# Making the first tile's branch products, y and transposed y in the end of the last attention unit

## The chip, the core and the metric

The kernel runs on one core of a Trainium2 chip. The metric is the device time of one execution in microseconds (us). The core's engines work side by side, each through a list of its own: PE (matrix multiplication, with PEld for the loading of weights), DVE (vector), ACT (activation functions), POOL (general purpose) and SP, which here only issues DMA transfers (its rows are called SPq). They wait for each other through semaphores.

## What is computed

One layer of a streaming encoder, for 2048 prompt rows and 8 x 16 sample rows of width 1024. Rows are normalized and projected; then come two kinds of attention, a differential softmax attention (4 heads) and a stick-breaking attention (8 heads, weights from a running product along the keys); then the two results are merged:

```python
oa = rms_norm(oa, subln_g) * (1.0 - lam_init)
ya = (oa.reshape(b, s, WIDTH_A) * jax.nn.silu(za)) @ w_branch_a
yb = (ob.reshape(b, s, WIDTH_B) * jax.nn.silu(zb)) @ w_branch_b
return (jax.nn.sigmoid(ga) * ya + jax.nn.sigmoid(gb) * yb) @ w_out
```

The merged rows are gated, added to the input and normalized. The sample rows also attend to caches of 512 keys and values for each of 8 sequences. Keys and values are outputs too.

Every product of high precision is made of three fp16 matmuls: each operand is cut into a high and a low half (`split`: the high half is a cast, on ACT or POOL, and the low half is what is left, on DVE, L294), and high x high, high x low and low x high are added up in PSUM.

## The kernel before, in words

There are three stages.

**Stage 0** normalizes the rows and writes them, transposed, to DRAM.

**Stage 1, attention.** Eight units (u = 0 to 7), each a head of the softmax kind or two heads of the stick-breaking kind, go over 17 tiles of 128 rows each: the sample tile first, then the 16 prompt tiles. A loop of 138 iterations (136 steps, and two more for what is left) issues the pieces of each: projections some tiles ahead, taken from one long list, the scores of this tile (`scores`), and the weighted sums of the values of the tile two steps back (`pv`). For a stick-breaking head a chunk of 512 keys goes through PE (L628, L629), two sigmoids on ACT (L119), a scan on DVE (L605), and for each stretch of 1024 keys a product on POOL (L611), a cast on ACT (L561), a subtraction on DVE (L562) and a transposing DMA into `wt` (L569), which PE then uses in L680 and L681. Unit 7 is of the stick-breaking kind, and its last tiles are the longest: 15 and 16 blocks of keys.

When the list of projections has run out, which happens some four iterations before the end, `early_work` makes another short list: the last of the branch weights, the handing out of buffers (`rest`), and `inputs` of the first two tiles of stage 2. It is spread evenly over the iterations that are left.

**Stage 2, the output.** The pools of stage 1 are closed, and their memory goes to the buffers of stage 2. Tile by tile:

- `inputs(t)` loads o, z (into two buffers, `hs0` and `hs1`) and the gates g, makes o * silu(z) on POOL (L1144), ACT (L119) and DVE (L1150, L1146), and splits it into `u16` (`hs2`).
- `turned` transposes u on PE (L1126, two groups of eight), and ACT copies it from PSUM (L1127).
- `branches` makes four products of 12 matmuls each (L1268, half j and branch br); DVE scales and gates each (L1270), POOL adds the two branches (L1272), and `finish` makes y: squares on ACT (L271), the scale in a few column operations on DVE, two splits, and `iy` (L1286).
- `turned_y` transposes y as `turned` does.
- `output` makes two products of 24 matmuls with `wo`, the cut w_out (L1309), and then the gate, the addition of x (L1317), the last normalization and the store (L1323).

In iteration n of the output loop stand the branches of tile n, `turned` of tile n + 1, `inputs` of tile n + 2, `output` of tile n - 1 and `turned_y` of tile n, interleaved by their stated costs with the pieces of the sample lane, `aside(n)`: the sample rows' attention to the caches (L727 loads, L734 transposing DMAs, L752 scores, L783 weighted sums), about five steps of it beside each of the first tiles. Ahead of the loop the eight pieces of w_out are loaded and cut (L1118, with two buffers, then L291 or L289 and L294).

PSUM has two banks for branch products and sigmoids of z (`mm`), three for scores and transposes (`s`), one `t` and two `o`.

A scheduler goes over all this: it keeps the order in which buffers are handed out, but may move an instruction ahead of others on its engine by its own estimate of time. So the compiled order of each engine is fixed, and it isn't that of the source. On one engine the instructions start in that order.

Of the kernel before, what the change touches and what calls it, by code (L numbers as in the profile page):

```python
# [16 lines left out]
F32 = mybir.dt.float32  # L17
F16 = mybir.dt.float16
# [3 lines left out]
ALU = mybir.AluOpType  # L22
# [3 lines left out]
P = 128  # L26
# [83 lines left out]
def layer_kernel(ctx: ExitStack, tc: tile.TileContext, a: dict):  # L110
# [74 lines left out]
    def bank(tag, dt=F32):  # L185
        return ps.tile([P, 512 if dt == F32 else 1024], dt, tag=tag, name=f"ps_{tag}", bufs=BANKS[tag])
# [26 lines left out]
    def scales(square, pool, name, n=1):  # L213

        tag = "sc" if n == 1 else f"sc{n}"
        kw = {} if n == 1 else dict(bufs=1)
        q = tiny.tile([P, n], F32, tag=tag + "_q", name="sc_q", **kw)
        V.tensor_scalar(out=q, in0=square, scalar1=2.0 ** -46, scalar2=None, op0=ALU.max)
        f = tiny.tile([P, n], I32, tag=tag + "_f", name="sc_f", **kw)
        V.tensor_scalar(out=f, in0=q.bitcast(I32), scalar1=24, scalar2=None, op0=ALU.logical_shift_right)  # L220
        e = tiny.tile([P, 2 * n], I32, tag=tag + "_e", name="sc_e", **kw)
        V.tensor_scalar(out=e[:, 0:n], in0=f, scalar1=-1.0, scalar2=204.0, op0=ALU.mult, op1=ALU.add)
        V.tensor_scalar(out=e[:, n : 2 * n], in0=f, scalar1=50.0, scalar2=None, op0=ALU.add)
        s = pool.tile([P, 2 * n], I32, tag=name, name=name)
        V.tensor_scalar(out=s, in0=e, scalar1=23, scalar2=None, op0=ALU.logical_shift_left)
        return s.bitcast(F32)
# [39 lines left out]
    def sum_squares(src, n, dst, width=1024, scale=1.0):  # L266

        for i in range(0, n, width):
            junk = tiny.tile([P, width], F16, tag="junk", name="junk", bufs=1)
            w = min(width, n - i)  # L270
            S.activation(out=junk[:, 0:w], in_=src[:, i : i + w], func=AF.Square, scale=scale,  # L271
                         accum_out=dst[:, i // width : i // width + 1])

    def add_up(acc, n):
        if n == 1:
            return acc[:, 0:1]
        col = tiny.tile([P, 1], F32, tag="col", name="col")
        V.tensor_reduce(out=col, in_=acc[:, 0:n], axis=AX.X, op=ALU.add)
        return col
# [6 lines left out]
    def split(hi, lo, src, s, on=None):  # L286

        if on is S:
            S.activation(out=hi, in_=src, func=AF.Identity, scale=s)  # L289
        elif on is G:  # L290
            G.tensor_scalar(out=hi, in0=src, scalar1=s, scalar2=0.0, op0=ALU.mult, op1=ALU.add)  # L291
        else:
            V.tensor_scalar(out=hi, in0=src, scalar1=s, scalar2=None, op0=ALU.mult)
        V.scalar_tensor_tensor(out=lo, in0=src, scalar=s, in1=hi, op0=ALU.mult, op1=ALU.subtract)  # L294
# [818 lines left out]
    L = {}  # L1113
# [8 lines left out]
    def transposed(x16, dst, half):  # L1122

        pt = bank("s", F16)
        for k in range(KT):
            T.transpose(pt[:, k * P : (k + 1) * P], x16[:, half, k * P : (k + 1) * P], id16)  # L1126
        S.copy(out=dst[:, half * KT : (half + 1) * KT, :], in_=pt.rearrange("p (k n) -> p k n", n=P))  # L1127
# [34 lines left out]
    def turned(st):  # L1162

        st["u"] = st["u"].bitcast(F16).rearrange("p (k n) -> p k n", n=P)
        for half in range(2):
            transposed(st["u16"], st["u"], half)


    tiles = list(range(NT - 1)) + [NT, NT - 1]
    states, begun = {}, []  # L1170
# [14 lines left out]
    def early_work():  # L1185


        free.extend(units[7]["bufs"])

        def first(t):  # L1190
            if "orms" not in L:
                L["orms"] = rsqrt(osums[:, 0:NT, :].rearrange("p t h -> p (t h)"), 4 * NT, P, con, "orms")
            states[t] = inputs(t)
            if t == tiles[0]:
                turned(states[t])

        def rest():
            L["g"], L["u"], (L["y"], L["y16"]) = free[0:4], free[4:6], free[6:8]

        return [branch_weight for _ in branch_weights] + [rest] + [lambda t=t: first(t) for t in tiles[0:2]]  # L1200

    for n in range(len(steps) + PV_LAG):
        made, qk, vs = [], [], []
# [30 lines left out]
    with ExitStack() as c2:  # L1234
# [21 lines left out]
            T.matmul(pg, sel[0:9, i * P : (i + 1) * P], gsm[0:9, :], start=True, stop=True)  # L1256
            return pg

        def branches(st):

            def half(j, br):
                c = slice(j * 512, (j + 1) * 512)
                g = st["g"][j][:, br, :]
                pb = bank("mm")
                n = 0
                for wi, ui in ((0, 0), (0, 1), (1, 0)):
                    for k in range(4):
                        T.matmul(pb, st["u"][:, ui * 8 + br * 4 + k, :], wb[br * 4 + k // 2 * 2 + j][:, wi, k % 2, :], start=(n == 0), stop=(n == 11))  # L1268
                        n += 1
                V.scalar_tensor_tensor(out=g, in0=pb, scalar=st["iu"], in1=g, op0=ALU.mult, op1=ALU.mult)  # L1270
                if br == 1:
                    G.tensor_tensor(out=g, in0=st["g"][j][:, 0, :], in1=g, op=ALU.add)  # L1272
                    if j == 1:
                        finish()

            def finish():
                acc = tiny.tile([P, 2], F32, tag="yacc", name="yacc")
                for j in range(2):
                    sum_squares(st["g"][j][:, 1, :], 512, acc[:, j : j + 1])
                sy = scales(add_up(acc, 2), unit, "sy")  # L1280
                y16 = L["y16"].bitcast(F16).rearrange("p (f n) -> p f n", f=2)
                for j in range(2):
                    c = slice(j * 512, (j + 1) * 512)
                    split(y16[:, 0, c], y16[:, 1, c], st["g"][j][:, 1, :], sy[:, 0:1], S)
                iy = unit.tile([P, 1], F32, tag="iy", name="iy")
                V.tensor_tensor(out=iy, in0=sy[:, 1:2], in1=s_o[:, 1:2], op=ALU.mult)  # L1286
                st["y16"], st["iy"] = y16, iy

            return [(2.6, lambda j=j, br=br: half(j, br)) for j in range(2) for br in range(2)]

        def turned_y(st):
            st["y"] = yT = L["y"].bitcast(F16).rearrange("p (k n) -> p k n", n=P)
            for half in range(2):
                transposed(st["y16"], yT, half)

        def output(t, st):
            box = {}

# [47 lines left out]
        load(out=fg, in_=a["final_g"].rearrange("(o d) -> o d", o=1).to_broadcast([P, D]))  # L1346
        for n in range(NT + 2):
            work = []
            if n <= NT:
                work += branches(states[tiles[n]])  # L1350
            if n + 1 <= NT:

                work.insert(2, (0.9, lambda n=n: turned(states[tiles[n + 1]])))
            if n + 2 <= NT:
                work.insert(5, (0.1, lambda n=n: states.update({tiles[n + 2]: inputs(tiles[n + 2])})))
            if n > 0:
                work += output(tiles[n - 1], states.pop(tiles[n - 1]))
            if n <= NT:
                work.append((0.9, lambda n=n: turned_y(states[tiles[n]])))
            interleave(work, aside(n))  # L1360

# [26 lines left out]
```

## Time and profile before

| | |
|---|---|
| median of 3 runs | 2374.07 us (2372.82 to 2374.98) |
| profiled execution | 2379.63 us, its span 2377.8 us |
| granted PE clock, mean of the span | 0.959 |
| PE busy | 2115.9 us (89%) |
| DVE busy | 1736.5 us (73%) |
| ACT busy | 1658.8 us (70%) |
| POOL busy | 749.0 us (32%) |
| last weighted sum of attention (L681) | 1823.02 us |
| first output product (L1309) | 1872.30 us |

Times inside the span count from its start. In the page's second part the span is cut into 40 slices of 59.4 us, and a digit gives the busy share of an engine in tenths; PEclk is the clock that was granted to PE. In a timeline a row has its start, its length, engine, line, operation, what it writes and reads, the count of merged instructions, and in brackets the idle time before it with what ended it. Lengths of pipelined matmuls overlap: the pace of a group is the distance from its start to that of the next. In a table by windows each engine has its busy time and the number of its instructions, and the last three columns are the granted clock, the share of the DMA engines' time and GB/s.

### The profile page before, as it was taken

How to read it: one execution, taken by the hardware profiler on the slowest of the kernel's cores; microseconds unless marked ns; L12 is line 12 of the kernel's file. 1: busy time of each engine (PE TensorE's matmuls, PEld its weight loads, DVE VectorE, ACT ScalarE, POOL GpSimd, SP SyncE). 2: the span in 40 equal slices, each digit the busy share in tenths (PEclk: the TensorE clock that was granted, in tenths of full speed). 3: DMA queues.
4: the chain of work that ended last, by engine and by line, in shares of the span. 5: the costliest groups of instructions: out<-in, count | busy, mean ns of one | idle time of the engine just before them, and what ended most of it. 6: DMA issues, size and time to landing. Idle time of an engine off the chain costs nothing. (4 is left out here: it accounts for less than half of the span.)

```text
span 2377.8 us, 42492 instructions
## 1 busy us (share of the span) xinstructions
PE 2115.9 (89%) x15136; PEld 1126.4 (47%) x15136; DVE 1736.5 (73%) x3647; ACT 1658.8 (70%) x3216; POOL 749.0 (32%) x604
## 2 busy tenths in 40 slices
PE   5779998998989899899999989999986779888998
PEld 2435554444545445445545544554543344444443
DVE  4868665779875667977667797777787777777654
ACT  3758767787886777877677787866776767766652
POOL 1833022345300233641023364103343333232322
PEclk7979999999999999999999999999997889999899
DMA  9668859887795878878687897866788999999421
GB/s 325 223 197 213 204 132 242 191 197 160 186 237 129 201 187 191 175 181 186 145 196 181 182 181 180 193 155 153 155 185 198 271 247 244 233 252 227 147 99 54
DMA packets 843573, 453.74 MB, mean 191 GB/s; under 512 B 538234, under 2 KB 786346, under 8 KB 842848
## 3 DMA queue, kind: packets, MB, share of 16 engines
q1 hardware_dynamic: 843360, 451.03, 77.0%
q8 instruction: 118, 1.93, 0.3%
q14 instruction: 95, 0.78, 0.1%
HBM read 249.80 MB, written 73.44 MB: 136 GB/s over the span
## 5 line engine op out<-in xcount | busy, mean ns | idle before, releaser
L611 POOL TENSOR_TENSOR sc_p<-sc_p,sc_n 128x127 f32<-128x127 f32 (+7 forms) x192 | 308.6, 1611 | 900.5 <-DVE sc_n L605 887.5
L426 PE MATMUL ps_mm<-wb,hs 128*128 128x512 f16 x1632 | 413.1, 381 | 0.2 <-DVE v L294 0.2
L426 PEld LDWEIGHTS <-hs 128*128 128x128 f16 x3120 | 271.9, 98 | 258.1 <-DMA hs<-hT_d 17.1
L426 PE MATMUL ps_mm<-wa,hs 128*128 128x512 f16 x1488 | 373.4, 383 | 15.1 <-DMA hs<-hT_d 15.1
L605 DVE TENSOR_TENSOR_SCAN sc_n<-ps_s,sc_n,zero_t 128x512 f32<-128x512 f32 x192 | 245.4, 1278 | 80.2 <-ACT ps_s L119 76.0
L628 PE MATMUL ps_s<-k,qst 128*128 128x512 f16 (+3 forms) x640 | 225.8, 354 | 45.4 <-DVE sc_n L605 38.7
L562 DVE TENSOR_TENSOR sc_n<-sc_p,sc_n 128x128 f16<-128x128 f32 (+7 forms) x192 | 224.4, 1172 | 54.4 <-ACT sc_n L561 53.8
L493 PEld LDWEIGHTS <-hs 128*128 128x128 f16 x1632 | 156.1, 98 | 183.1 <-DVE qst L521 5.6
L119 ACT ACTIVATE sc_p<-ps_s,usc 128x512 f32<-128x512 f32 (+3 forms) x320 | 202.8, 634 | 43.0 <-PE ps_s L629 31.5
L629 PE MATMUL ps_s<-k,qst 128*128 128x512 f16 (+3 forms) x640 | 225.9, 354 | 0.0
L561 ACT CAST sc_n<-sc_p 128x128 f16<-128x128 f32 (+7 forms) x192 | 154.6, 807 | 76.6 <-POOL sc_p L611 76.4
L680 PE MATMUL ps_o<-v,wt 128*128 128x128 f16 x1088 | 173.4, 226 | 33.8 <-DMA wt<-sc_n 33.5
L119 ACT ACTIVATE ps_s<-ps_s,usc 128x512 f32<-128x512 f32 (+3 forms) x328 | 197.9, 603 | 0.0
L493 PE MATMUL ps_t<-wa,hs 128*128 128x512 f16 x816 | 193.8, 382 | 3.2 <-DVE qst L521 3.2
L493 PE MATMUL ps_t<-wb,hs 128*128 128x512 f16 x816 | 190.3, 381 | 2.3 <-DVE qst L521 2.2
L1309 PE MATMUL ps_o<-wo,wa 128*128 128x512 f16 x816 | 189.4, 386 | 0.7 <-ACT wa L1127 0.7
L681 PE MATMUL ps_o<-v,wt 128*128 128x64 f16 x1088 | 158.8, 198 | 0.0
L680 PEld LDWEIGHTS <-wt 128*128 128x128 f16 x1088 | 105.9, 102 | 100.7 <-DMA wt<-sc_n 45.3
L547 DVE TENSOR_SCALAR_CACHE_REDUCE sc_p<-ps_s,usc 128x512 f32<-128x512 f32 (+3 forms) x160 | 106.2, 664 | 48.0 <-PE ps_s L629 29.0
L547 DVE TENSOR_SCALAR_CACHE_REDUCE sc_n<-ps_s,usc 128x512 f32<-128x512 f32 (+3 forms) x160 | 106.3, 664 | 43.0 <-PE ps_s L629 18.7
L605 DVE TENSOR_TENSOR_SCAN sc_n<-ps_s,zero_t 128x128 f32<-128x128 f32 (+3 forms) x128 | 104.2, 814 | 43.7 <-ACT ps_s L119 38.9
L459 POOL TENSOR_TENSOR rot<-pr,rope 128x256 f32<-128x256 f32 x68 | 61.7, 908 | 223.3 <-ACT pr L440 181.7
(336 smaller groups left out, 4591.7 us busy)
## 6 DMA issues: line engine op xcount, KB each, us to landing
hs<-hT_d SPq DMA_DIRECT2D x130, 512.0 KB, 4.3
g_d<-gt SPq DMA_DIRECT2D x68, 256.0 KB, 4.3
wb<-g_d SPq DMA_DIRECT2D x34, 512.0 KB, 5.7
out_dram<-pr SPq DMA_DIRECT2D x204, 64.0 KB, 2.1
wide<-in_w_ada_dram SPq DMA_DIRECT2D x12, 1024.0 KB, 7.3
z_d<-pr SPq DMA_DIRECT2D x136, 64.0 KB, 2.1
o_d<-o SPq DMA_DIRECT2D x136, 64.0 KB, 2.2
hs<-z_d SPq DMA_DIRECT2D x17, 512.0 KB, 5.6
```

What stands on the lines that cost most here:

```text
L119: i = S.activation(**kw)
L426: T.matmul(box["p"], box["h"][:, hi, k, :], U["w"][k][:, wi, :], start=(n == 0), stop=(n == 3 * KT - 1))
L493: T.matmul(box["g"][:, 0:gw], box["h"][:, hi, k, :], U["wg"][k // per][:, k % per, wi, :], start=(j == 0), stop=(j == 3 * KT - 1))
L547: V.tensor_scalar(out=dst[:, lo : lo + n], in0=p[:, 0:n], scalar1=sc_pos, scalar2=None, op0=ALU.mult, op1=ALU.max, accum_out=job["mx"][:, ...
L562: V.tensor_tensor(out=lo, in0=src, in1=hi, op=ALU.subtract)
L605: V.tensor_tensor_scan(out=dst[:, lo : lo + n][:, ::-1], data0=src[:, 0:n][:, ::-1], data1=zero_t[:, 0:1].to_broadcast([P, n]), initial=fi ...
L611: G.tensor_tensor(out=p[:, 0:m], in0=p[:, 0:m], in1=n[:, 1 : m + 1], op=ALU.mult)
L628: T.matmul(p[:, 0:n], qst[:, c, :], kk[:, c, 0:n], start=True, stop=False)
L629: T.matmul(p[:, 0:n], qst[:, 2 + c, :], kk[:, c, 0:n], start=False, stop=not diag)
L680: T.matmul(po[:, c * P : (c + 1) * P], wt[:, wj, :], vt[:, c, :, :], start=first, stop=False)
L681: T.matmul(po[:, c * P : c * P + 64], wt[:, nb + wj, :], vt[:, c, 0, :], start=False, stop=last)
L1309: T.matmul(po, st["y"][:, yi * 8 + k, :], wo[j * 4 + k // 2][:, wi, k % 2, :], start=(n == 0), stop=(n == 3 * KT - 1))
```

## The change

`branches` and `turned_y` move out of the output stage, unchanged but for taking the weights and the scale from `L`, so that the end of the attention loop can call them. `early_work` gets five more pieces, the four branch products of the first tile (the last with `finish`) and its `turned_y`, so that its list is nine long and not four. Since the list is spread over the iterations that are left, the pieces that it had before come earlier too: `inputs` of the first tile two iterations earlier (in step 134, beside the scores of tile 14), and `inputs` of the second in step 135. In the output loop iteration 0 has no branches and no `turned_y`.

```diff
+        def early(i):
+
+            if i == 0:
+                L["first"] = [fn for _, fn in branches(states[tiles[0]])] + [lambda: turned_y(states[tiles[0]])]
+            L["first"][i]()
+
         def rest():
             L["g"], L["u"], (L["y"], L["y16"]) = free[0:4], free[4:6], free[6:8]
 
-        return [branch_weight for _ in branch_weights] + [rest] + [lambda t=t: first(t) for t in tiles[0:2]]
+        return [branch_weight for _ in branch_weights] + [rest] + [lambda t=t: first(t) for t in tiles[0:2]] \
+            + [lambda i=i: early(i) for i in range(5)]
...
         for n in range(NT + 2):
             work = []
-            if n <= NT:
+            if 0 < n <= NT:
                 work += branches(states[tiles[n]])
...
-            if n <= NT:
+            if 0 < n <= NT:
                 work.append((0.9, lambda n=n: turned_y(states[tiles[n]])))
             interleave(work, aside(n))
```

The matmuls, their shapes and their count stay the same; 29,541 rows stand on PE in both. In the compiled order of the changed kernel the instructions stand as follows, and the prediction uses these places:

- PE: the 16 transposes of the first tile's u stand ahead of the last nine chunks of scores (before: behind all of them). Between the tenth and the ninth chunk from the end stand, with these transposes, 58 matmuls of weighted sums. Two of the branch products stand ahead of the third chunk from the end, and one ahead of each of the last two. The transposes of y, and of the second tile's u, stand behind the first 48 of the last 80 weighted sums.
- DVE: the first tile's L1150 and L1146 and its split stand ahead of the last nine scans; the second tile's, and the scalings of the four products (L1270), among the nine; the column operations that make y's scale stand ahead of the last L562.
- ACT: the sigmoids of the first tile's z and gates, its squares, its split and its copies stand ahead of the last nine pairs of score sigmoids.
- POOL: the second tile's L1144 and the two additions of y stand among the last L611.
- SP: the loads of the second and third tile's o and z stand among the last transposing DMAs; the first load of w_out still comes behind the last of these.
- From the row that is branch product 1 of the fourth tile on, PE has started the same set of instructions in both kernels. Just ahead of it the changed order has the second tile's output product before the third tile's branch products.

64 lines of the change are left out of this document (32 added, 32 removed).

## The prediction

> **What bounds the kernel now.** I read the page first, then a table by windows over the seam between attention and output, then the timelines of PE, DVE, ACT and SP there. The page says that PE carries the kernel, except at its ends and at a dip three quarters through.
>
> ```profile
> span 2377.8 us, 42492 instructions
> ...
> PE   5779998998989899899999989999986779888998
> ```
>
> The 31st to 33rd of the 40 slices (some 1783 to 1962 us) are the dip: 6, 7, 7. The change works there, so the windows (busy us of PE, PEld, DVE, ACT, POOL; then clock, DMA share, GB/s):
>
> ```profile
> 1780.00:1800.00 20.00, 11.28 (x87) 6.02 (x86) 19.20 (x20) 17.06 (x28) 11.91 (x6) 0.80 0.80 141
> 1800.00:1820.00 20.00, 8.89 (x90) 6.71 (x89) 16.59 (x25) 15.90 (x23) 8.34 (x5) 0.59 0.77 161
> 1820.00:1840.00 20.00, 16.76 (x104) 8.88 (x102) 12.00 (x28) 9.20 (x11) 4.63 (x4) 0.85 0.95 284
> 1840.00:1860.00 20.00, 5.96 (x24) 2.51 (x23) 16.90 (x26) 12.67 (x18) 9.20 (x7) 0.66 1.03 270
> 1860.00:1880.00 20.00, 20.00 (x139) 9.65 (x137) 13.80 (x26) 14.79 (x20) 5.16 (x5) 1.00 1.09 285
> 1880.00:1900.00 20.00, 15.58 (x134) 8.22 (x132) 16.90 (x41) 14.81 (x22) 5.52 (x4) 0.94 0.97 251
> 1900.00:1930.00 30.00, 21.20 (x157) 9.55 (x156) 20.74 (x36) 17.23 (x31) 13.10 (x8) 0.84 1.00 230
> ```
>
> Two different stretches lie here. From 1780 to 1820, the end of attention, PE is half idle, but DVE is busy for 35.8 of 40 us: the scans set the pace, and PE's idle time is free only to work that asks nothing of DVE and ACT. From 1840 to 1860 nobody is full; that is a chain. PE's timeline names it:
>
> ```profile
> 1823.02 0.19 PE L681 MATMUL ps_o<-v,wt 128*128 128x64 f16 x1
> 1826.46 4.60 PE L1268 MATMUL ps_mm<-wa,wa 128*128 128x512 f16 x14 [3.24 <-POOL hs L1144]
> ...
> 1841.01 0.59 PE L1268 MATMUL ps_mm<-wb,wa 128*128 128x512 f16 x2
> 1854.76 0.61 PE L1126 MATMUL ps_s<-id,wa 128*128 128x128 f16 x4 [13.15 <-ACT wa L289]
> ...
> 1867.20 1.90 PE L752 MATMUL ps_s<-dks,qpad 128*32 128x512 f16 x29
> ...
> 1872.30 1.89 PE L1309 MATMUL ps_o<-wo,wa 128*128 128x512 f16 x8
> ...
> 1874.47 8.80 PE L1309 MATMUL ps_o<-wo,wa 128*128 128x512 f16 x40
> 1883.10 2.97 PE L1268 MATMUL ps_mm<-wa,wa 128*128 128x512 f16 x13
> ```
>
> Attention's last weighted sum ends at 1823.2. The first tile's 48 branch matmuls run from 1826.46 to 1841.4, PE waits 13.15 us for y's split, then come the second tile's branch products and, to 1883.1, the first tile's output. The change takes the 48 matmuls and that wait out of this stretch. From 1823.2 to 1883.1 are 59.9 us, so what there is to win looks like 20 to 30 us.
>
> **What it costs, step by step.** (a) *The scores are held up.* In the changed order the last nine chunks of scores stand behind 58 weighted sums and the first tile's 16 transposes. The last 16 of the 58 need a `wt` that comes no sooner than now:
>
> ```profile
> 1786.90 0.61 PE L628 MATMUL ps_s<-k,qst 128*128 128x512 f16 x1
> ...
> 1799.49 0.29 PE L680 MATMUL ps_o<-v,wt 128*128 128x128 f16 x1 [0.41 <-DMA wt<-sc_n]
> ...
> 1800.77 0.61 PE L628 MATMUL ps_s<-k,qst 128*128 128x512 f16 x1
> ...
> 1820.53 1.90 PE L1126 MATMUL ps_s<-id,hs 128*128 128x128 f16 x16
> ```
>
> The first of the nine chunks now starts at 1786.90. The sixteen sums start at 1799.49 and are through at 1800.77; 1.9 us of transposes put the chunk at 1802.7, 15.8 us later. The transposes' own operand is no later than that: ACT makes the sigmoids, squares and the high half, and DVE the rest.
>
> ```profile
> 1787.98 0.69 ACT L119 ACTIVATE sc_p<-ps_s,usc 128x512 f32<-128x512 f32 x1 [0.47 <-PE ps_s L629]
> ...
> 1806.22 1.15 ACT L119 ACTIVATE ps_mm<-hs 128x512 f32<-128x512 f32 x2
> 1807.27 2.03 ACT L119 ACTIVATE wb<-wb 128x1024 f32<-128x1024 f32 x2
> ...
> 1816.21 1.17 ACT L289 ACTIVATE hs<-hs,su 128x1024 f16<-128x1024 f32 x1
> ...
> 1842.95 1.00 ACT L1127 COPY wb<-ps_s 128x1024 f16<-128x1024 f16 x1
> ```
>
> From 1806.22 to the high half's end at 1817.4 are 11.2 us here, with attention's casts and the second tile's sigmoids between. In the changed order this work takes the place of the score sigmoids that start at 1787.98; it then ends at 1799.2, and the low half on DVE (1.28, below) at 1800.5. So the wait for `wt` covers it, by 0.3 us; without that cover the delay grows by what it is late. The last row, a copy of transposes, is used in (f).
>
> (b) *DVE has more to do among the nine.*
>
> ```profile
> 1785.69 2.46 DVE L562 TENSOR_TENSOR sc_n<-sc_p,sc_n 128x1024 f16<-128x1024 f32 x1
> ...
> 1793.03 1.20 DVE L562 TENSOR_TENSOR sc_n<-sc_p,sc_n 128x1024 f16<-128x1024 f32 x1
> ...
> 1795.28 1.75 DVE L562 TENSOR_TENSOR sc_n<-sc_p,sc_n 128x896 f16<-128x896 f32 x1
> ...
> 1806.38 2.66 DVE L605 TENSOR_TENSOR_SCAN sc_n<-ps_s,sc_n,zero_t 128x512 f32<-128x512 f32 x2
> 1808.96 1.10 DVE L1150 SCALAR_TENSOR_TENSOR hs<-ps_mm,orms,hs 128x128 f32<-128x128 f32 x4
> 1809.98 0.68 DVE L1146 TENSOR_TENSOR hs<-hs,ps_mm 128x512 f32<-128x512 f32 x1
> ...
> 1817.41 1.28 DVE L294 SCALAR_TENSOR_TENSOR hs<-hs,su,hs 128x1024 f16<-128x1024 f32 x1 [1.85 <-ACT hs L289]
> ...
> 1831.55 0.74 DVE L1270 SCALAR_TENSOR_TENSOR wb<-ps_mm,iu,wb 128x512 f32<-128x512 f32 x1
> ```
>
> Now the last scan ends at 1809.04, 22.1 us behind the first chunk's start. Added are four scalings (4 x 0.74 = 2.96), the second tile's 1.10 + 0.68, and its low half, 1.28: 6.0 us. Two L562 that now lie inside (1.20 and 1.75) are done during the hold-up: 3.0 less. The last scan ends at 1802.7 + 22.1 + 3.0 = 1827.8. The 48 matmuls themselves, 10.4 us at the pace of the 40 in the row at 1874.47 (8.63 us to the next start, 0.216 each), lie between the chunks in PE time that is idle (19.8 us from 1780 to 1820); I charge nothing for them, and if DVE didn't cover them, it would be at most those 10.4. The Trainium skill, "TensorE: Matmul & The Clock Gate", section on HAM oscillation, says that idle gaps of some 3.4 us halve PE's clock. The trace agrees in kind (granted 0.59 from 1800 to 1820); by the page the 48 would take about 20.7 us in place of 10.4, still mostly beside the scans, and the sum would be the same or some us longer.
>
> (c) *To the last weighted sum.* Now 14.2 us pass from the last scan to it (1809.04 to 1823.21). The two additions of y on POOL stand ahead of the last L611:
>
> ```profile
> 1840.06 1.27 POOL L1272 TENSOR_TENSOR wb<-wb 128x512 f32<-128x512 f32 x1
> ```
>
> One of them costs 1.27; y's column operations on DVE stand where the first tile's stand now, so they come out even. 1827.8 + 14.2 + 1.3 = 1843.3: attention ends 20.1 us later. That is a bound from above for a DVE that is fed without pause, since it takes the hold-up whole. From below, DVE's added 6.0 us and POOL's 1.27 remain, 7.3, if the hold-up is caught up whole; it can't be less, as nothing leaves DVE. I take 20.1, since the nine chunks are one chain on DVE.
>
> (d) *w_out.* Its loads go to memory that attention has held:
>
> ```profile
> 1823.25 0.90 SPq L1118 DMA_DIRECT2D x<-in_w_out_dram  x2
> 1826.79 0.43 SPq L727 DMA_DIRECT2D dc<-in_cache_a_k_dram  x1
> ...
> 1862.25 1.28 DVE L294 SCALAR_TENSOR_TENSOR wo<-x,s_w,wo 128x1024 f16<-128x1024 f32 x1
> ```
>
> The first load is issued at 1823.25, right behind the last weighted sum, and the eighth piece is cut at 1863.5, 40.3 us later; now nobody waits for it, as the first output comes at 1872.3. The second tile's branch products (from 1843.3, 12 us) and the first half of the output are through before it in the changed kernel, so **w_out is late next**: 1843.3 + 40.3 = 1883.6, and 20 of the second half's matmuls (4.3 us) end at 1887.9. Now that point is 1883.1: the change is 4.8 us behind, with the wait for y gone.
>
> (e) *To where both orders meet again*, ahead of the fourth tile's branches:
>
> ```profile
> 1887.81 0.74 PE L783 MATMUL ps_t<-dwt,v16c 128*128 128x16 f16 x24 [0.26 <-DMA dwt<-dsc]
> ...
> 1927.45 5.30 PE L1268 MATMUL ps_mm<-wa,wb 128*128 128x512 f16 x14 [8.65 <-DVE hs L1150]
> ```
>
> Now 44.35 us, of which PE works 31.1 (15.58 + 21.20 of the two windows, less 3.1 before 1883.1 and 2.5 behind 1927.45). The changed order has 1.0 less (y's transposes are done). It runs straight into the second tile's output, but then meets the sample lane's weighted sums. Now 18.7 us pass between the lane's last scores (1869.1) and these (1887.81); the changed order has only 9 + 24 matmuls between (7.1 us), so PE waits 11.6. That is 30.1 + 11.6 = 41.7 us, 2.6 less than now: 4.8 - 2.6 = 2.2 behind.
>
> (f) Two L562 at 2.46 and not 1.20, since POOL's additions and L1144 now run among them: 2.5, between none and eight such (10). And ACT's copy of the second y (1.00) has to wait for the last read of the first in the same buffer, with nothing beside it on PE: 1.0. Sum: 2.2 + 2.5 + 1.0, **5.7 us later.** The profiled execution, 2379.63, would become 2385.3; it lies 5.56 over the median, so against the runs' 2374.07 I forecast 2379.8.
>
> **The rivals.** *The hold-up is caught up.* DVE uses the wait for casts, and the end of attention comes 10 us later, not 20: then w_out is cut at 1873.5, the output ends at 1877.8 (5.3 ahead), and with 2.6 from (e) and nothing lost in (f) it is 7.9 faster: 2366.2. For it: DVE's 4.2 idle us and two casts done early. Against: DVE has 35.8 of 40 us of work now. The Trainium skill, "PSUM — Partial Sum Buffer", section on engine and sequencer instructions, has matmuls start in program order; that speaks against this rival, since a chunk of scores can't pass the transposes. The row at 1854.76 agrees: branch products stood 13.15 us behind it.
>
> *The sample lane sets the pace.* Its first cache load comes at 1826.79 and goes 20 us later, and the DMA share of 0.95 to 1.09 from 1820 to 1900 leaves it little to catch up with. It decides where more than the sum's 11.6 us are lost at L783: the whole 20.1, less 11 (some 3 MB, the second and third tile's o and z and the third's gates, of 0.5 MB each, loaded early, at 270 GB/s), gives 9 to 10 later: 2384. For it: the share. Against: PE worked 20 of 20 us beside it.
>
> *It comes out even*, 2374: the delay of (c) lies between, at 14 us, where 15.3 us less of waiting and (e) and (f) balance it. *The change doesn't do what it says*: the compiled order speaks against that.
>
> **How the numbers follow.** A measurement of this kernel tells about 0.2% (4.7 us) from no change. Forecast 0.33 (from 2 to 8 us later, a third of it within 0.2%), lane 0.22, caught up 0.33, even 0.10, no effect 0.02. So slower 0.44, same 0.23, faster 0.33. The range goes down to the bound of 7.3 us in (c) (the output ends at 1875.1, 8.0 ahead, and with (e) 10.6: 2363.5, and 1.5 for a shorter wait at L783), and up to the lane's case with half of the 10 us of (f): 2362 to 2390; the forecast's own is 2376 to 2382.
>
> **What would show it.** Right: the ninth chunk from the end starts near 1802, the last L681 ends near 1843, the first L1118 right behind it; PE waits for wo's L294 in the first output and at L783. Wrong: the last L681 before 1835, or no wait in the output, or waits beyond the fourth tile that differ by more than 5 us, since I count both kernels as equal from there.

## The result, and the profile after

| | before | changed |
|---|---|---|
| median of 19 runs each | 2376.55 us (2367.45 to 2385.73) | 2381.58 us (2376.90 to 2387.19) |
| ratio | | 1.0024, 95% interval 1.0014 to 1.0034 |
| profiled execution | 2379.63 us, span 2377.8 us | 2386.86 us, span 2385.1 us |

The changed kernel takes 0.24% longer: 5.7 us of 2376.55, between 3.3 and 8.1. Both profiled executions lie above the medians, and they don't start the seam at the same time, so their spans can't simply be subtracted. The last fixed point ahead of the seam is the first chunk (384 keys) of the scores of tile 14's second head, which I call **the mark**. The timelines of PE, first of before, then of the changed kernel:

```profile
1780.94 0.32 PE L628 MATMUL ps_s<-k,qst 128*128 128x384 f16 x1 [0.84 <-DVE sc_n L605]
```

```profile
1776.00 0.32 PE L628 MATMUL ps_s<-k,qst 128*128 128x384 f16 x1 [0.84 <-DVE sc_n L605]
...
1794.29 0.29 PE L680 MATMUL ps_o<-v,wt 128*128 128x128 f16 x1 [3.20 <-DMA wt<-sc_n]
...
1795.33 1.06 PE L1126 MATMUL ps_s<-id,hs 128*128 128x128 f16 x8
1796.41 0.88 PE L1126 MATMUL ps_s<-id,hs 128*128 128x128 f16 x8
1797.13 0.38 PE L628 MATMUL ps_s<-k,qst 128*128 128x512 f16 x1
...
1804.48 4.53 PE L1177 MATMUL ps_mm<-wa,wa 128*128 128x512 f16 x14 [0.41 <-DVE sc_n L604]
...
1829.85 0.61 PE L1126 MATMUL ps_s<-id,wa 128*128 128x128 f16 x4 [3.35 <-ACT wa L289]
...
1835.37 0.19 PE L681 MATMUL ps_o<-v,wt 128*128 128x64 f16 x1
```

The mark comes 4.94 us earlier in the changed kernel's execution; a second profile of the changed kernel (e8, below) has it 3.1 us later than this one, so such differences are there without any change. Everything that follows is counted from it. The ninth chunk from the end (1797.13) stands behind the weighted sums that wait for `wt` and behind the sixteen transposes: 21.1 us behind the mark, where it was 6.0. The last L681 is 59.4 behind the mark, where it was 42.1.

The same windows as before, in the changed kernel (counted from the mark they lie 4.94 us further on; busy us of PE, PEld, DVE, ACT, POOL; granted clock, DMA share, GB/s):

```profile
1780.00:1800.00 20.00, 9.80 (x97) 7.46 (x97) 13.19 (x22) 13.52 (x21) 5.32 (x3) 0.58 0.71 155
1800.00:1820.00 20.00, 15.73 (x77) 6.92 (x76) 17.48 (x27) 18.09 (x29) 11.89 (x7) 0.91 0.35 79
1820.00:1840.00 20.00, 12.29 (x116) 8.98 (x117) 14.71 (x29) 11.99 (x17) 9.29 (x6) 0.66 0.78 195
1840.00:1860.00 20.00, 15.67 (x58) 6.08 (x57) 13.32 (x25) 7.93 (x11) 9.13 (x6) 0.83 0.95 266
1860.00:1880.00 20.00, 12.64 (x56) 5.03 (x55) 12.48 (x17) 9.35 (x10) 3.03 (x2) 0.74 1.00 271
1880.00:1900.00 20.00, 14.04 (x88) 6.10 (x85) 9.10 (x18) 9.70 (x13) 5.03 (x4) 0.98 0.98 246
1900.00:1930.00 30.00, 21.77 (x202) 10.60 (x202) 24.04 (x45) 21.51 (x35) 7.68 (x5) 0.73 0.90 236
```

From 1780 to 1800 DVE works 13.19 us of 20 and not 19.20: that is the hold-up, seen from the engine that it starves. The hole of 1840 to 1860, where PE worked 5.96 us, is filled (15.67). But two new ones follow: 12.64 from 1860 to 1880, where PE had worked 20.00, and 14.04 from 1880 to 1900. And the DMA share is 0.35 from 1800 to 1820 (0.77 before): with the scores held up, only three of attention's transposing DMAs (L569) are issued there and not five. What PE waits for in the new holes, in the changed kernel's timeline:

```profile
1864.49 0.59 PE L1316 MATMUL ps_o<-wo,wa 128*128 128x512 f16 x2 [2.13 <-POOL wo L291]
...
1872.14 1.01 PE L1316 MATMUL ps_o<-wo,wa 128*128 128x512 f16 x2 [3.03 <-POOL wo L291]
...
1875.35 5.79 PE L1316 MATMUL ps_o<-wo,wa 128*128 128x512 f16 x18 [2.19 <-ACT wo L289]
...
1881.53 0.61 PE L1126 MATMUL ps_s<-id,wa 128*128 128x128 f16 x8 [0.39 <-ACT wa L1127]
...
1901.21 5.65 PE L1177 MATMUL ps_mm<-wa,wa 128*128 128x512 f16 x14 [6.78 <-DVE hs L1150]
...
1921.81 2.72 PE L752 MATMUL ps_s<-dks,qpad 128*32 128x512 f16 x21 [3.67 <-DMA dks<-k16c]
...
1931.02 6.10 PE L1177 MATMUL ps_mm<-wa,wb 128*128 128x512 f16 x14 [4.38 <-DVE hs L1150]
```

First it waits for w_out, inside the first output product, which ends at 1881.14. Then the third tile's branch products (1901.21) wait for L1150. That row needs care: they don't read the z that L1150 works on. They write a PSUM bank `mm`, and ahead of them in the order of the two banks stand the sigmoids of the *fourth* tile's z, which L1150 has to read first. ACT's timeline tells why these are late, before and changed:

```profile
1875.56 0.83 ACT L119 ACTIVATE dsc<-dsc,nm 128x640 f32<-128x640 f32 x1 [0.92 <-DVE nm L575]
...
1878.61 1.12 ACT L119 ACTIVATE ps_mm<-hs 128x512 f32<-128x512 f32 x2
```

```profile
1893.64 1.15 ACT L289 ACTIVATE k16c<-dc,s_c 128x1024 f16<-128x1024 f32 x1 [2.38 <-DMA dc<-in_cache_b_k_dram]
...
1896.34 0.83 ACT L119 ACTIVATE dsc<-dsc,nm 128x640 f32<-128x640 f32 x1 [0.26 <-DVE nm L575]
...
1899.39 1.12 ACT L119 ACTIVATE ps_mm<-hs 128x512 f32<-128x512 f32 x2
```

In both kernels the sigmoids stand on ACT behind the sample lane's first exponentials (`dsc`), and these come 94.6 us behind the mark before and 120.3 in the changed kernel. The last cast of keys ahead of them (1893.64) waited for its cache load. The lane began 24.3 us later (its first cache load 45.9 and 70.2 behind the mark), and nearly all of that arrives at the third tile's branch products (102.2 and 125.2 behind the mark). By the fourth tile (1931.02) the changed kernel is 155.0 us behind the mark, before 146.5.

### The profile page after: what moved, and what is told of

The parts are those of the page before. It is cut to its first block, busy times and chain, and to the rows that moved or that the text cites. A ratio compares the mean times of both kernels' runs of the same rounds, so it can differ in the third digit from the quotient of the medians.

```text
span 2385.1 us, 42473 instructions
## 1 busy us (share of the span) xinstructions
PE 2118.3 (89%) x15136; PEld 1127.4 (47%) x15136; DVE 1734.9 (73%) x3647; ACT 1658.9 (70%) x3216; POOL 745.0 (31%) x604
## 5 line engine op out<-in xcount | busy, mean ns | idle before, releaser
L611 POOL TENSOR_TENSOR sc_p<-sc_p,sc_n 128x127 f32<-128x127 f32 (+7 forms) x192 | 309.2, 1615 | 898.0 <-DVE sc_n L605 882.4
L426 PEld LDWEIGHTS <-hs 128*128 128x128 f16 x3120 | 271.4, 98 | 254.0 <-DMA hs<-hT_d 14.5
L426 PE MATMUL ps_mm<-wa,hs 128*128 128x512 f16 x1488 | 371.4, 381 | 13.2 <-DMA hs<-hT_d 13.1
L562 DVE TENSOR_TENSOR sc_n<-sc_p,sc_n 128x128 f16<-128x128 f32 (+7 forms) x192 | 224.1, 1171 | 53.5 <-ACT sc_n L561 52.8
L681 PE MATMUL ps_o<-v,wt 128*128 128x64 f16 x1088 | 158.1, 197 | 0.0
L605 DVE TENSOR_TENSOR_SCAN sc_n<-ps_s,zero_t 128x128 f32<-128x128 f32 (+3 forms) x128 | 104.3, 815 | 45.1 <-ACT ps_s L119 39.8
```

Of the source, the lines that this page charges most:

```text
L426: T.matmul(box["p"], box["h"][:, hi, k, :], U["w"][k][:, wi, :], start=(n == 0), stop=(n == 3 * KT - 1))
L562: V.tensor_tensor(out=lo, in0=src, in1=hi, op=ALU.subtract)
L605: V.tensor_tensor_scan(out=dst[:, lo : lo + n][:, ::-1], data0=src[:, 0:n][:, ::-1], data1=zero_t[:, 0:1].to_broadcast([P, n]), initial=fi ...
L611: G.tensor_tensor(out=p[:, 0:m], in0=p[:, 0:m], in1=n[:, 1 : m + 1], op=ALU.mult)
L681: T.matmul(po[:, c * P : c * P + 64], wt[:, nb + wj, :], vt[:, c, 0, :], start=False, stop=last)
```

## The experiments

All are compared with the kernel before on the same chip. The five columns of places are us behind the mark in that kernel's own profile.

| kernel | last L681 ends | lane's first exponential | first output ends | fourth tile's branches | end | ratio of the time to before (95%) |
|---|---|---|---|---|---|---|
| before | 42.3 | 94.6 | 102.3 | 146.5 | 596.9 | 1 |
| changed | 59.6 | 120.3 | 105.1 | 155.0 | 609.1 | 1.0024 (1.0014 to 1.0034) |
| e8, changed again | 58.7 | 118.6 | 103.7 | 153.0 | 603.0 | 1.0034 (1.0021 to 1.0047) |
| e1, behind the scores (1) | 47.0 | 102.7 | 102.4 | 147.9 | 597.6 | 1.0009 (0.9999 to 1.0018) |
| e2, early inputs only | 62.7 | 111.3 | 110.5 | 157.7 | 609.8 | 1.0061 (1.0049 to 1.0074) |
| e3, changed, third buffer | 58.8 | 112.1 | 91.9 | 153.2 | 609.6 | 1.0046 (1.0033 to 1.0060) |
| e4, before, third buffer | 42.1 | 96.9 | 101.0 | 144.7 | 594.4 | 1.0000 (0.9987 to 1.0013) |
| e5, behind the scores (2) | 56.1 | 112.0 | 104.3 | 154.9 | 602.5 | 1.0017 (1.0007 to 1.0027) |
| e6, changed, lane from 1 | 58.7 | 121.0 | 113.4 | 127.2 | 594.3 | 0.9980 (0.9967 to 0.9993) |
| e7, before, lane from 1 | 42.8 | 107.6 | 91.3 | 125.1 | 580.0 | 0.9916 (0.9900 to 0.9932) |
| e9, pieces behind the loop | 42.8 | 94.7 | 99.5 | 146.0 | 593.9 | 0.9984 (0.9972 to 0.9995) |
| e10, e9 with lane from 1 | 42.8 | 118.4 | 98.6 | 127.1 | 589.2 | 0.9961 (0.9945 to 0.9976) |
| e11, before, more traffic | 42.4 | 97.7 | 104.8 | 149.6 | 598.3 | 1.0018 (1.0006 to 1.0030) |
| e12, changed, inputs ahead | 58.2 | 115.7 | 114.6 | 155.9 | 600.6 | 1.0010 (0.9996 to 1.0023) |

**Is it the hold-up of the scores? e1, e5 and e9.** In e1 the first tile's transposes move to the piece of its first branch product, and two empty pieces push that behind the last scores. The inputs of the second tile are issued ahead of it and into the same buffer, so the first tile's products are made from the second tile's u; its times are those of a kernel that does so.

```diff
-            if t == tiles[0]:
-                turned(states[t])
...
             if i == 0:
+                turned(states[tiles[0]])
...
-            + [lambda i=i: early(i) for i in range(5)]
+            + [lambda: None] * 2 + [lambda i=i: early(i) for i in range(5)]
```

> The first tile's u transposes, its branch products and its y stay early, but all stand behind the last chunk of scores on PE (its inputs still come two iterations early). Theory 'hold-up' (the changed kernel is late because the last nine chunks of scores stand behind the first tile's transposes on PE, and w_out starts only when attention ends): the ninth chunk from the end follows the tenth as closely as before, the last L681 comes 0 to 4 us later than before and not 12 to 20, the first output ends 5 to 9 us ahead of before, and the time is 4 to 9 us under before. Rival 'load' (it is the added work on DVE, ACT and POOL in the end of attention, wherever it stands): the last L681 stays 8 us or more behind before, and the time is 3 to 8 us over before, like the changed kernel. Rival 'transfers' (the output stage goes at the pace of its DMA, which starts when attention ends): the time is within 2 us of before, since attention ends where it did and the bytes are the same.

The ninth chunk from the end follows the mark at 5.5 us, and attention ends 4.7 later than before: so far the theory holds. But the time is not under before; it is 0.1% over it or equal. Taken alone that would speak for "transfers", as the first output ended where it did.

e5 issues the second tile's inputs behind the transposes, with three empty pieces:

```diff
+                turned(states[tiles[0]])
+                first(tiles[1])
...
-        return [branch_weight for _ in branch_weights] + [rest] + [lambda t=t: first(t) for t in tiles[0:2]] \
-            + [lambda i=i: early(i) for i in range(5)]
+        return [branch_weight for _ in branch_weights] + [rest] + [lambda: first(tiles[0])] \
+            + [lambda: None] * 3 + [lambda i=i: early(i) for i in range(5)]
```

> The early branch products as in the changed kernel, but the first tile's u transposes and the second tile's inputs are issued behind the last scores (the first tile's inputs stay in the iteration of tile 14). In the compiled order no chunk of scores stands behind a transpose any more; the 48 branch products stand among the last 64 weighted sums. Theory 'hold-up': the last L681 comes 0 to 6 us later than before, counted from tile 14's diagonal chunk, and not 17 as in the changed kernel; with w_out as the next to be late, the time is 4 to 9 us under before. Rival 'lane' (the end of the kernel goes with the start of the sample lane, whose loads begin when attention ends; what PE does meanwhile is made up or lost before the fourth tile): the time follows the last L681, so it is 0 to 4 us over before although the first output ends earlier. 'Load' (the added work itself): the last L681 stays 8 us or more behind before.

The last score starts 3 us later than before, not 18, yet attention ends 13.8 us later. PE in e5:

```profile
1827.08 0.29 PE L680 MATMUL ps_o<-v,wt 128*128 128x128 f16 x1 [4.16 <-DMA wt<-sc_n]
...
1827.23 1.04 PE L1177 MATMUL ps_mm<-wb,wa 128*128 128x512 f16 x2
...
1834.46 0.59 PE L1177 MATMUL ps_mm<-wb,wa 128*128 128x512 f16 x2
```

The last weighted sums wait for their transposed weights until 1827.08, and then stand among the last 24 branch products, which take PE from 1827.23 to 1835.05. So "load" has its share: attention ends late without a hold-up of scores too, as soon as the early work stands ahead of the last weighted sums. The time follows that end, 0.17% over before. e9 takes both away. The five pieces are issued behind the attention loop, the list in it has its old length:

```diff
-        return [branch_weight for _ in branch_weights] + [rest] + [lambda t=t: first(t) for t in tiles[0:2]] \
-            + [lambda i=i: early(i) for i in range(5)]
+        L["late"] = [lambda i=i: early(i) for i in range(5)]
+        return [branch_weight for _ in branch_weights] + [rest] + [lambda t=t: first(t) for t in tiles[0:2]]
...
+    for fn in L["late"]:
+        fn()
     c01.close()
```

> The changed kernel's five early pieces are issued behind the last iteration of the attention loop, and the list inside the loop has its old four pieces, so that the inputs and u's transposes stand where they stand in the kernel before. No chunk of scores stands behind a transpose; the branch products come right behind the last weighted sum. Theory 'hold-up, then the lane' (the change loses by ending attention 16 to 17 us later, and gains by taking y out of the lane's way): last L681 within 1 us of before from tile 14's diagonal chunk, no wait of 13 us for y's transposes, first output's end 8 to 15 us ahead of before, and the time 8 to 17 us under before. Rival 'the end goes with the end of attention alone' (the lane starts there, and nothing won before the fourth tile is kept): the time is within 2 us of before. Rival 'the early branches cost it wherever they stand': 2 us or more over before.

Attention ends where it did, and the time is 0.16% under before; against the changed kernel's two ratios that is 0.40% or 0.50% less, 9.5 to 12 us. So what the early inputs and pieces do to the end of attention costs the changed kernel some 10 us of time; that much of the mechanism is shown. That the 17 us alone do it isn't: the orders behind attention differ too. The gain is smaller than expected because the wait for y shrinks from 13.15 and doesn't go (e9's PE):

```profile
1844.27 1.92 PE L1126 MATMUL ps_s<-id,wa 128*128 128x128 f16 x12 [8.75 <-ACT wa L289]
```

y's chain is as long as it was, and the transposes now stand on PE ahead of work that could have covered them.

**Are the early inputs enough? e2** leaves the branch products in the output loop and only lengthens the list:

```diff
         return [branch_weight for _ in branch_weights] + [rest] + [lambda t=t: first(t) for t in tiles[0:2]] \
+            + [lambda: None for i in range(5)]
```

> The kernel before with five empty pieces added to the list at the end of attention: the inputs of the first two tiles come two iterations earlier, as in the changed kernel, but the branch products and y stay in the output loop of the source. Theory 'hold-up': the transposes of u stand ahead of the last nine chunks of scores again, so the hold-up of some 15 us is there and the time is 2 to 8 us over before, as with the whole change. Rival 'the early branches themselves cost it' (their scalings and y among the last scans): within 2 us of before. (The scheduler may move the branch products of the first tile up by itself; then both say as with the whole change, and the run says that the earlier inputs alone are enough for it.)

0.61% over before, some 14.5 us: more than the whole change, and more than the 2 to 8 us expected. The scheduler pulls the branch products to the same places by itself, behind the early inputs; it also puts the second tile's transposes and 24 of its branch products among the last weighted sums (attention ends 20.4 us later). What costs, then, is where the inputs stand, not that the pieces were written down early.

**Is w_out what is late next? e3 and e4** let every third piece of w_out use a buffer that is idle by then:

```diff
-                st = s2.tile([P, D], F32, tag="x", name="x", bufs=2)
+                st = gts if len(wo) % 3 == 0 else s2.tile([P, D], F32, tag="x", name="x", bufs=2)
```

> The changed kernel with a third staging buffer for the pieces of w_out (the buffer of final_g, idle by then), so that one piece is loaded beside attention and three can be under way. Theory 'hold-up', step 'w_out is late next': PE's waits for wo ahead of and in the first output product (0.76, 1.01, 0.21, 2.13, 3.03 and 2.19 us in the changed kernel, 9.3 together) fall under 4 us, the first output ends 4 to 7 us earlier, and the time falls 3 to 6 us against the changed kernel, to about that of before. Rival 'transfers': the same bytes follow, so the waits move to the caches (L752, L783) or to the third tile's inputs, and the time falls by no more than 2 us (the 0.5 MB moved ahead at about 250 GB/s).

> The kernel before with the same third staging buffer. Theory 'hold-up': nobody waits for w_out in the kernel before (the eighth piece is cut at 1863.5, the first output comes at 1872.3), so the time stays within 2 us. Rival 'transfers': 2 us less, as much as in the changed kernel. A gain as large as in the changed kernel, over 3 us, would say that w_out is not what the change made late.

In e3 the eighth piece is cut 86.4 us behind the mark and not 100.6, and the first output ends 13.2 us earlier. The time is not shorter; it is 0.46% over before. PE in e3:

```profile
1858.62 1.01 PE L1316 MATMUL ps_o<-wo,wa 128*128 128x512 f16 x2 [3.01 <-POOL wo L291]
...
1893.56 6.00 PE L1177 MATMUL ps_mm<-wa,wa 128*128 128x512 f16 x14 [7.13 <-DVE hs L1150]
```

Of the waits for w_out some 4 us are left, and the third tile waits 7.13 us for L1150, as in the changed kernel; by the fourth tile 1.8 of the 13.2 us remain. w_out is a wait on PE's path, but the time doesn't hang on it. e4 agrees: no difference.

**Does the lane carry the delay? e6, e7 and e12.** In e6 and e7 iteration 0 of the output loop has no pieces of the lane:

```diff
-            interleave(work, aside(n))
+            interleave(work, aside(n) if n else [])
```

> The changed kernel with the sample lane's first pieces issued in iteration 1 of the output loop, none in iteration 0. On ACT the third tile's sigmoids of z now stand ahead of the lane's third cast of a cache, not behind its sixth. Theory 'lane through ACT's order' (in the changed kernel PE waits 6.78 us at the third tile's branches for L1150, whose sigmoids stand on ACT behind casts that wait for cache loads): that wait falls under 2 us, the third tile's branches start 5 us or more earlier, and the time falls 3 to 8 us against the changed kernel. Rival 'transfers' (the bytes set the pace, in whatever order): the waits only move to L752 and L783, the lane's last L783 comes no earlier, and the time is within 2 us of the changed kernel, or over it. Prediction as put on record (wait at L783, gone by the fourth tile): no change of the time either.

> The same edit in the kernel before. 'Lane through ACT's order': there the third tile's L1150 isn't waited for, but the fourth tile's is (8.65 us), behind the lane's casts as well; the gain is smaller than in the changed kernel, 0 to 4 us. 'Transfers': within 2 us, or slower by what the lane starts later.

Both gain far more than any theory allowed. e6 is 0.5% shorter than the changed kernel on the same chip (2372.32 us, and 2384.67 in e8), and e7 is 0.84% under before, 2358.21 us against 2377.31: **faster than both kernels**, with an edit that has nothing to do with the change. In e6 the wait of 6.78 us is gone and the third tile's branches start 80.4 us behind the mark, not 125.2. The first rows of the third and of the fourth tile's branch products in e6:

```profile
1855.90 3.65 PE L1177 MATMUL ps_mm<-wa,wa 128*128 128x512 f16 x14
...
1902.66 3.18 PE L1177 MATMUL ps_mm<-wa,wb 128*128 128x512 f16 x14 [0.58 <-DVE hs L1150]
```

In e7 PE's order is another one, and that shows best what the kernel before lacked. Its PE timeline:

```profile
1843.66 5.47 PE L1268 MATMUL ps_mm<-wa,wb 128*128 128x512 f16 x14 [5.31 <-DVE hs L1150]
...
1856.30 1.06 PE L1126 MATMUL ps_s<-id,wa 128*128 128x128 f16 x16
```

All of the second tile's branch products stand ahead of y's transposes here, and after a wait of 5.31 us they cover the chain for which before waits 13.15 us. So the wait that the change goes after can be covered from behind, without touching attention. How e7's 19 us divide between this and the sigmoids that now stand ahead of the lane's exponentials isn't separated.

The table adds two things. A late lane alone doesn't make the kernel late: e7's first exponential comes 13.0 us later than before's, and its end 16.9 earlier. And with the lane in iteration 1 the change costs more, not less: e6 takes 14.1 us longer than e7 on the same chip (2372.32 and 2358.21 us), with the fourth tiles only 2.1 us apart and the ends 14.3. So the later end of attention can cost time beyond the fourth tile too; by which wait, no run here settles.

e12 is the narrow test of ACT's order: the lane keeps its iterations, but in iteration 1 the branch products, the transposes and the fourth tile's inputs are issued ahead of it.

```diff
+            if n == 1:
+                for _, fn in work[0:6]:
+                    fn()
+                work = work[6:]
             interleave(work, aside(n))
```

> The changed kernel, with iteration 1 of the output loop in two parts: its branch products, the third tile's transposes and the fourth tile's inputs are issued first, and only then the lane's pieces together with the first tile's output. The lane stays in its iterations. On ACT the fourth tile's sigmoids of z now stand ahead of the lane's first two exponentials, not behind them. Theory 'ACT's order' (the third tile's branch products take the PSUM banks behind these sigmoids, the sigmoids stand behind the lane's exponentials, and these come with the lane's first scores, so a later end of attention reaches the third tile whole): the wait of 6.8 us ahead of the third tile's branch products goes, they start 20 us or more earlier, and the time falls 5 us or more against the changed kernel. Rival 'the lane's pace itself' (its loads, casts and scores, which stay): the waits move behind the third tile, to L752 and L783, and the time stays within 3 us of the changed kernel.

PE in e12:

```profile
1859.57 3.20 PE L1177 MATMUL ps_mm<-wa,wa 128*128 128x512 f16 x14
...
1881.88 1.01 PE L752 MATMUL ps_s<-dks,qpad 128*32 128x512 f16 x2 [6.59 <-DMA dks<-k16c]
...
1909.03 0.79 PE L783 MATMUL ps_t<-dwt,v16c 128*128 128x16 f16 x24 [3.89 <-DMA dwt<-dsc]
...
1925.08 3.24 PE L752 MATMUL ps_s<-dks,qpad 128*32 128x512 f16 x26 [6.70 <-DMA dks<-k16c]
```

The third tile's products start at once, 80.8 us behind the mark, and the waits have moved to L752 and L783. The fourth tile comes no earlier than in the changed kernel (155.9 and 155.0). That is the rival, "the lane's pace itself", as far as the fourth tile; with the lane in iteration 0, ACT's order is only the place where its delay meets PE. The time lies 3 to 6 us nearer to before than the changed kernel's two ratios; these were not measured beside it, and the interval touches no difference, so whether something is won further on is left open.

**e10** joins e9's and e7's edits.

> The same, and the lane's first pieces issued in iteration 1 of the output loop. Theory: both edits take away the same wait (y behind the lane's casts on ACT), so together they give little more than the lane's edit alone in the kernel before: 15 to 22 us under before, within 4 us of that one. If what they win adds up, 25 to 35 us under before.

It is a miss: 0.39% under before (9.3 us), where e7 is 0.84% under on another chip. y's transposes are back on PE ahead of the cover, and PE in e10 waits:

```profile
1849.12 1.22 PE L1126 MATMUL ps_s<-id,wa 128*128 128x128 f16 x8 [12.49 <-ACT wa L289]
```

**e8** is the changed kernel once more, unedited.

> The changed kernel once more, for a second profile of it beside the others of this call. Counted from tile 14's diagonal chunk, the last L681 lies 17 us behind that of before again, the first output's end 2 to 4 us, the fourth tile's branches 7 to 10 us, and the end 9 to 13 us. If the end lies only about 5 us behind, as the medians do, the profile on record was one of the changed kernel's longer executions.

The first four places agree with the first profile within 2.1 us, the end within 6.1: the changed kernel is 6.4 us behind before at the fourth tile and 6.1 at the end. The changed kernel's first profile, 12.2 us behind at the end, was one of its longer executions.

**e11** doesn't answer its question:

```diff
+            if 3 <= n <= 6:
+                load(out=hT_d[0][:, 1], in_=hT_d[0][:, 0])
             interleave(work, aside(n))
```

> The kernel before with four copies of 0.5 MB from DRAM to DRAM added, one each in iterations 3 to 6 of the output loop; their result is not used. 'Transfers set the pace' of the output stage (DMA share 0.93 to 1.06 from 1820 to 2200): 2 MB at about 245 GB/s are 8 us, and the time is 6 to 10 us over before. If PE with its waits for single steps of the lane and the tiles sets it, and the share is only high: 0 to 3 us over.

Nothing waits for these copies, and the scheduler moved all four up into attention, to 1512 to 1528 us of the span; its 0.18% over before is the time with the copies there. Whether the bytes set the pace of the output stage stays open; e7 alone says that with the same bytes, and attention ending where it did, 19 us can go. e11 is of use in another way: behind the mark it is the kernel before, unchanged, and its fourth tile comes 3.1 us later. Single differences of less than that in the table say nothing.

## Why the forecast was right, and where it was not

The forecast was 5.7 us (2379.8 against 2374.07); the runs give 5.7 (3.3 to 8.1). The sum came out, but one of its terms has the wrong sign. On before's clock (4.94 us added to the changed kernel's):

| step | forecast | measured |
|---|---|---|
| (a) ninth chunk from the end | 1802.7 | 1802.1 |
| (b) last scan ends | 1827.8 | 1830.1 |
| (c) last L681 ends | 1843.3 | 1840.5 |
| (d) w_out cut; first output ends | 1883.6; 1887.9 | 1881.5; 1886.1 |
| (e) from there to the fourth tile's branches | 41.7 | 49.9 |
| fourth tile, against before | 5.7 with (f) | 8.5 and 6.4 |

(a) was right in size and in mechanism. The Trainium skill, "PSUM — Partial Sum Buffer", section on engine and sequencer instructions, has matmuls start in program order, and the trace agrees: the chunk at 1797.13 starts behind the last transpose, although nothing of it depends on u.

(b) and (c) missed in opposite directions and come out 2.8 us early together. DVE's rows in the changed kernel, among the last scans and behind them:

```profile
1808.61 0.75 DVE L1179 SCALAR_TENSOR_TENSOR wb<-ps_mm,iu,wb 128x512 f32<-128x512 f32 x1 [1.41 <-PE ps_mm L1177]
...
1813.86 1.98 DVE L562 TENSOR_TENSOR sc_n<-sc_p,sc_n 128x1024 f16<-128x1024 f32 x1
...
1818.93 2.95 DVE L294 SCALAR_TENSOR_TENSOR hs<-hs,su,hs 128x1024 f16<-128x1024 f32 x1
...
1822.47 2.65 DVE L605 TENSOR_TENSOR_SCAN sc_n<-ps_s,sc_n,zero_t 128x512 f32<-128x512 f32 x2
1825.04 1.20 DVE L562 TENSOR_TENSOR sc_n<-sc_p,sc_n 128x1024 f16<-128x1024 f32 x1
...
1829.26 1.21 DVE L562 TENSOR_TENSOR sc_n<-sc_p,sc_n 128x1024 f16<-128x1024 f32 x1
```

The last L562 in before:

```profile
1814.08 1.21 DVE L562 TENSOR_TENSOR sc_n<-sc_p,sc_n 128x1024 f16<-128x1024 f32 x1
```

The last scan is 2.3 us later than forecast. From its end to the end of the last L681 it is 10.4 us and not 15.5. Two L562 stand behind the last scan, where before had three with the first tile's L1150 among them, but that makes DVE's part only 0.9 us shorter (5.35, 6.25 before); the larger part, from the last L562 to the last L681, is 5.1 us and not 7.9. There before has three transposing DMAs in a row (issued from 1812.33 on) and u's sixteen transposes (1820.53). The rival that DVE catches up would have needed an end 10 us later, not 17. The 48 branch products, charged with nothing, cost little: DVE waits 1.41 us for the first of them (1808.61). The rule on HAM oscillation in the Trainium skill, "TensorE: Matmul & The Clock Gate", is that long idle gaps throttle PE's clock, and the prediction worked out half pace for all 48 from it, beside its own sum; the trace agrees for few of them: the granted clock is 0.58 from 1780 to 1800, but 0.91 from 1800 to 1820, where the row at 1804.48 has fourteen at 0.32 us each, and the later ones go at 0.216.

(d) was right to within 2 us, and e3 shows that it doesn't decide: with w_out 14 us earlier the time doesn't fall.

**(e) is the step that failed.** I let PE run straight from the first output into the second and put one wait, 11.6 us, at the lane's weighted sums (L783). PE doesn't wait there at all. It waits 6.78 us for L1150 ahead of the third tile's products, 3.67 for the lane's keys and 4.38 for L1150 again, 14.8 us in all. I had counted the distance from the lane's *scores* as fixed, and looked at who uses them; I didn't look at what stands behind the lane's exponentials on ACT, nor at who holds the two `mm` banks. The term was to be 2.6 us less than before's 44.35 and is 5.5 more (49.3 in e8, 5.0 more).

(f) has two parts. Its 2.5 us, for two L562 at 2.46, belong to the scans: there one L562 takes 1.98 us, the other four among the scans and behind them 1.20 or 1.21, and the second tile's low half takes 2.95 and not the 1.28 of the sum. That is about 2.4 us together, so the size is right, though most of it falls on another instruction. Its 1.0, for ACT's copy of the second y, shows as a wait of 0.39 us (1881.53) inside the measured 49.9. Beyond the fourth tile the kernels run alike (6.4 to 6.1 in e8; 8.5 to 12.2 in the first profile, within the 5 us that I allowed).

Of the rivals, "the sample lane sets the pace" was the nearest in mechanism: e12 shows the lane's delay arriving at the fourth tile, and e6 a fourth tile 27.8 us earlier without the lane in iteration 0. Its price, 9 to 10 us, lies above the interval of the runs, and its place, L783, was as wrong as mine. So the total was right in part by luck. Up to the end of the first output the forecast, with the 2.5 us of (f) that belong there, had the changed kernel 7.3 us behind, and it was 3.0; from there to the fourth tile it was to win back 1.6, and it lost 5.5.

Read by e9, the change is two things: y out of the way of the lane (worth 0.16%), and attention 17 us longer with the orders that follow from it (0.40% or more lost).

## What to carry to other kernels

Work that is pulled into the tail of a stage stands, on every engine's own list, ahead of something of that stage: before moving it, find the longest chain there (here scans on DVE fed by scores on PE) and ask what the moved work puts in front of it. When a stage's end moves, follow the *next* consumer that starts from nothing at that end (here the lane's cache loads), through the order of the engines and the rings of PSUM banks, and not only the buffer that is late first; and don't take the first place where the delay is gone for the end of it (e6 and e7). A wait on PE may be cheaper to cover from behind, by letting independent work pass it, than to remove from the front: moving the lane's start by one iteration, which let it pass, gave 0.84% (how much of it by this cover is open), and the change lost 0.24%.

## What the runs showed of the hardware

A releaser in a wait row can name a tile that the waiting instruction never reads: `hs L1150` ahead of a branch product is the reader of the PSUM bank that the product is to overwrite. It took the order of the `mm` banks to see it.

Profiled executions differ ahead of the seam by as much as the effect: the mark lies between 1775.50 and 1781.65 us in the fourteen profiles of this case (thirteen kernels, almost the same up to there), and for the changed kernel alone at 1776.00 and 1779.11. Counting from it brought differences between the same places of the two profiles of the changed kernel down to 2.1 us as far as the fourth tile.
